# Newton steps of all inverse square roots moved from VectorE to GpSimd in a two-layer decoder

## The chip, the core and the metric

The kernel runs on one core of one Trainium2 chip. The metric is the device time of one execution in microseconds. A core has five engines that run their own instruction streams side by side and wait for one another by semaphores: TensorE (PE in the profile, with PEld for its weight loads), VectorE (DVE), ScalarE (ACT), GpSimd (POOL) and SyncE (SP), which here issues the DMAs.

## The reference, cut to what matters

The model has two pre-norm layers on 256 tokens of width 2048, with 16 heads of 128. Layer A is latent attention: a projection gives query and key/value latents and a gate, the latents are normalised and projected up per head, and queries and keys are normalised again before the scores. Layer B is plain attention here (one block of 256 keys) with a linear position bias, and with normalised queries and keys. All of these norms are

```python
def rms_norm(x, g):
    xf = x.astype(jnp.float32)
    y = xf * lax.rsqrt(jnp.mean(xf * xf, axis=-1, keepdims=True) + EPS)
    return (y * g.astype(jnp.float32)).astype(x.dtype)
```

The kernel has one inverse square root per token and norm to compute, a few numbers on each of the 128 partitions: 2, 6, 8 or 12 columns.

## The kernel before, in words

Every product is made of three passes (high times high, and two mixed ones) over parts of the operands. A weight block `wr` comes in by DMA; ScalarE rounds it to its high part `wh` (line 146) and VectorE subtracts that to get the low part `wl` (line 150, 128 x 1024 numbers in most cases). There are three buffers for `wl`, four for `wh`. TensorE's order is written out: a planner (`ordered`) merges a main list of projections with a side list of attention steps, and `chain` ties each matmul to the one ahead of it. So TensorE takes its work in one fixed order and, when an operand is late, waits. The order on the other engines is set by the compiler's scheduler, which estimates what is ready; each engine takes its own instructions strictly in the order that it was given.

The inverse square root is the function `rsqrt`. Two integer instructions make a first guess from the bits of the number (lines 303 and 304, here called the seed), then three Newton steps of three instructions follow (lines 306 to 308), each depending on the one before. It is called 19 times:

- `token_scale`, once for each layer (2 columns): the factor per token, copied to `r_a` or `r_b`, from which `diag` and the matmul `ps_r` make the factors by row.
- `lat_norm` (6 columns), once: the norms of the latents. After it VectorE scales `sf` (line 552), and TensorE transposes that (`ps_lt`).
- `kv_done` in `group_a` (12 columns), once for each of the 8 groups of two heads of layer A. After it VectorE makes `rp`, `tok`, `ra` and `rb` out of the projections in PSUM (lines 636 to 515), which TensorE transposes (`ps_ta`).
- `n_done` in `group_b` (8 columns), twice for each of the 4 groups of four heads of layer B. After it VectorE makes `tok` (line 786), which is transposed by DMA and split.

In layer A the projections follow each other as: query block (two `wl` of 768), key/value block (one `wl` of 1024), the rest of one gate (three `wl` of 1024) and the start of the next gate (one `wl` of 1024). The first is announced by the transposes `ps_ta`. The softmax of two heads of the group before (`sm`, `mn`, `ri`, `pz`) lies on VectorE and ScalarE in between.

Of the kernel before, what the change touches and what calls it, by code (L numbers as in the profile page):

```python
# [26 lines left out]
ALU = mybir.AluOpType  # L27
# [65 lines left out]
def trunk(ctx: ExitStack, tc, xT, gains, cst, w_in_a, w_q_up, w_kv_up, w_out_a, w_in_b, w_out_b, outT):  # L93
    nc = tc.nc
# [204 lines left out]
    def rsqrt(v, n, tag):  # L299

        y = wk.tile([P, n], F32, tag=tag + "y", name="rs_y")
        t = wk.tile([P, n], F32, tag=tag + "t", name="rs_t")
        nc.vector.tensor_scalar(y.bitcast(I32), v.bitcast(I32), 1, None, op0=ALU.logical_shift_right)
        nc.vector.tensor_scalar(y.bitcast(I32), y.bitcast(I32), -1.0, float(0x5F3759DF), op0=ALU.mult, op1=ALU.add)
        for _ in range(3):
            nc.vector.tensor_tensor(t, v, y, op=ALU.mult)
            nc.vector.scalar_tensor_tensor(t, t, -0.5, y, op0=ALU.mult, op1=ALU.mult)
            nc.vector.scalar_tensor_tensor(y, t, 1.5, y, op0=ALU.add, op1=ALU.mult)
        return y

    def split_x(c, gcol):
# [21 lines left out]
    def token_scale(ssq, lay, out, needs, more):  # L333


        def f():
            ps = work("ps_st")
            for t in range(2):
                matmul(ps[:, t * P:(t + 1) * P], ssq[:, t * P:(t + 1) * P], ones, start=True, stop=True)
            v = one.tile([P, 2], F32, name="rv_" + lay)  # L340
            nc.vector.tensor_scalar(v, ps[:, :2 * P:P], 1.0 / DM, EPS, op0=ALU.mult, op1=ALU.add)
            r = out["r"] = one.tile([P, 2], F32, name="r_" + lay)
            nc.vector.tensor_copy(r, rsqrt(v, 2, "x"))
            more()

        def g():
            pr = work("ps_r")
            d = wk.tile([P, S], F32, tag="og", name="diag")
            for t in range(2):
                nc.vector.tensor_scalar(d[:, t * P:(t + 1) * P], ident, out["r"][:, t:t + 1], None, op0=ALU.mult)  # L350
            matmul(pr[:, :S], ones, paired(d), start=True, stop=True)
            rows = out["rows"] = one.tile([P, S], F32, tag="rr", name="rr_" + lay)
            nc.vector.tensor_copy(rows, pr[:, :S])

        a = Step(f, 436, 5500, needs, bank=True)
        return a, Step(g, 436, 1500, [a], bank=True)
# [178 lines left out]
    def lat_norm():  # L535
        st = one.tile([P, 2, 3], F32, name="lat_st")
        v = one.tile([P, 2, 3], F32, name="lat_v")
        parts = ((0, QR), (QR, KVR), (QR + KVR, ROPE))
        for t in range(2):
            for i, (o, n) in enumerate(parts):  # L540
                sq = wk.tile([P, 512], F32, tag="gx", name="sq")
                nc.scalar.activation(sq[:, :n], lat[t][:, o:o + n], AF.Square,  # L542
                                     accum_out=st[:, t, i:i + 1])
        for i, (o, n) in enumerate(parts):
            nc.vector.tensor_scalar(v[:, :, i], st[:, :, i], 1.0 / n, EPS, op0=ALU.mult, op1=ALU.add)
        r = rsqrt(v.rearrange("p a b -> p (a b)"), 6, "l")
        krz = wk.tile([P, 384], F32, tag="sm", name="krz", bufs=3).rearrange("p (t a d) -> p t a d", t=2, a=3)
        nc.vector.memset(krz, 0.0)
        rp = wk.tile([P, 2, 1, ROPE], F32, tag="rp", name="rp", bufs=1)
        for t in range(2):  # L550
            for i, (o, n) in enumerate(parts[:2]):
                nc.vector.tensor_scalar(lat[t][:, o:o + n], lat[t][:, o:o + n], r[:, 3 * t + i:3 * t + i + 1], None,
                                        op0=ALU.mult)
            o = parts[2][0]
            nc.scalar.activation(rp[:, t, 0], lat[t][:, o:o + ROPE], AF.Copy, scale=r[:, 3 * t + 2:3 * t + 3])
        rope_of(rp, 2, 1, krz[:, :, 1:2])
        lat_st["krz"] = krz
# [42 lines left out]
    def group_a(g):  # L600
# [13 lines left out]
        def kv_done(a):  # L614
            st = z["st"]
            z["v"] = vh, vl, v1 = v_tiles()
            for t in range(2):
                v = a[t].rearrange("p (h d) -> p h d", h=2)
                for h in range(2):
                    sq = wk.tile([P, P], F32, tag="sqa", name="sqa", bufs=1)  # L620
                    nc.scalar.activation(sq, v[:, h, :P], AF.Square, accum_out=st[:, 1, t, h:h + 1])
                if t == 0:
                    split_v(vh[:, :2], vl[:, :2], v[:, :, P:], None)
                else:
                    nc.scalar.copy(v1[:, :2], v[:, :, P:])
            sf = st.rearrange("p a b c -> p (a b c)")
            var = wk.tile([P, 12], F32, tag="ga_v", name="ga_v")
            nc.vector.tensor_scalar(var[:, :8], sf[:, :8], 1.0 / P, EPS, op0=ALU.mult, op1=ALU.add)
            nc.vector.tensor_scalar(var[:, 8:], sf[:, 8:], 1.0 / ROPE, EPS, op0=ALU.mult, op1=ALU.add)
            f = rsqrt(var, 12, "ga").rearrange("p (a b c) -> p a b c", a=3, b=2)  # L630
            rp = wk.tile([P, 2, 2, ROPE], F32, tag="rp", name="rp", bufs=1)
            for t in range(2):
                tk = z["tok", t] = wk.tile([P, 512], F32, tag="tok", name="tok", bufs=4)
                q = z["q"][t].rearrange("p (h d) -> p h d", h=2)
                k = a[t].rearrange("p (h d) -> p h d", h=2)
                nc.vector.tensor_tensor(rp[:, t], q[:, :, P:], f[:, 2, t].unsqueeze(2).to_broadcast([P, 2, ROPE]),
                                        op=ALU.mult)
                for i, src in ((0, q), (1, k)):
                    nc.vector.tensor_tensor(tk[:, 256 * i:256 * (i + 1)].rearrange("p (h d) -> p h d", h=2), src[:, :, :P],
                                            f[:, i, t].unsqueeze(2).to_broadcast([P, 2, P]), op=ALU.mult)  # L640
            z["rope"] = rope_of(rp, 0, 2)
# [300 lines left out]
```

## Time and profile before

| | us |
|---|---|
| median of 3 runs | 756.62 |
| lowest and highest | 755.7, 757.58 |
| the profiled execution | 756.45 |
| its span, first to last instruction | 754.7 |
| outside the span | 1.75 |
| TensorE busy in the span | 745.3 (99%) |
| VectorE busy | 576.7 (76%) |
| ScalarE busy | 488.7 (65%) |
| GpSimd busy | 0.2 |

The share of busy time says which engine has work at all; whether a millisecond or a nanosecond on another engine reaches the end is told by TensorE's own waits, which the rows below list.

### The profile page before, as it was taken

To read this page: it belongs to the slowest core of one execution; us is meant where nothing else is said; L and a number is where in the kernel's file an instruction comes from. 1 tells how busy PE (TensorE), PEld (TensorE's weight loads), DVE (VectorE), ACT (ScalarE), POOL (GpSimd) and SP (SyncE) were. 2 spreads that over 40 slices of the span, in tenths; PEclk is the share of its full clock that TensorE was granted. 3 is DMA by queue.
4 is the path that set the end of the run, shared out by engine and by line. 5 is a ranking of instruction groups with operands and counts; after the bars stand their busy time and mean duration, and the time that the engine had idled before them with its cause. 6 is when DMAs were issued, how large, how long until landed. Compare 5 with 4: busy or idle time off the path is not lost.

```text
span 754.7 us, 14125 instructions
## 1 busy us (share of the span) xinstructions
PE 745.3 (99%) x5246; PEld 707.1 (94%) x5246; DVE 576.7 (76%) x1207; ACT 488.7 (65%) x1025; POOL 0.2 (0%) x4
## 2 busy tenths in 40 slices
PE   8999999999999999999999999999999999999997
PEld 7999999999999999998889988998889988899997
DVE  6888899999998596765787767886788857887552
ACT  7767888888877575445666556675567666674331
POOL 0000000000000000000000000000000000000000
PEclk9999999999999999999999999999999999999999
DMA  9866666666657966666877768876787677877761
GB/s 296 263 182 182 169 184 161 184 170 158 182 178 192 280 209 211 195 181 211 227 224 187 194 216 228 246 187 195 203 237 219 190 215 214 235 197 219 232 223 43
DMA packets 137973, 153.19 MB, mean 203 GB/s; under 512 B 47280, under 2 KB 94768, under 8 KB 137904
## 3 DMA queue, kind: packets, MB, share of 16 engines
q1 hardware_dynamic: 137760, 152.27, 70.4%
q8 instruction: 41, 0.67, 0.4%
q14 instruction: 28, 0.23, 0.1%
q10 hardware_dynamic: 144, 0.02, 0.0%
HBM read 139.68 MB, written 2.10 MB: 188 GB/s over the span
## 4 chain that ended last, share of the span: by engine, by line
PE 91%; DVE 4%; DMA 2%; ACT 1%; issue 1%; SPq 0%; DVEq 0%; ACTq 0%
PE acc L198 84%; PE ps_s L198 4%; DVE wl L150 2%; PE ps_o L198 2%; PE ps_ta L201 1%; DMA c_sb<-cst 1%; DMA wr<-w_in_a 1%; ACT wh L146 1%; DMA sm<-pz 0%; ACT sq L542 0%; DVE xt L724 0%; SPq L132 0%; PE ps_lt L201 0%; DVE xt L865 0%; DVE xl L314 0%
## 5 line engine op out<-in xcount | busy, mean ns | idle before, releaser
L146 ACT ACTIVATE wh<-wr 128x1024 fp32r<-128x1024 f32 (+3 forms) x265 | 287.9, 1091 | 161.8 <-PE acc L198 134.9
L150 DVE TENSOR_TENSOR wl<-wr,wh 128x1024 fp32r<-128x1024 f32 (+3 forms) x265 | 314.3, 1189 | 90.3 <-PE acc L198 58.1
L198 PE MATMUL acc<-wh,xh 128*128 128x512 f32 (+1 forms) x448 | 169.0, 377 | 1.2 <-ACT wh L146 1.2
L198 PE MATMUL acc<-wl,xh 128*128 128x512 f32 (+1 forms) x448 | 167.7, 374 | 0.8 <-DVE wl L150 0.8
L198 PE MATMUL acc<-wh,xl 128*128 128x512 f32 (+1 forms) x448 | 167.4, 374 | 0.0
L198 PE MATMUL acc<-xh,wh 128*128 128x256 f32 x512 | 142.3, 278 | 0.0
L198 PE MATMUL acc<-ogh,wh 128*128 128x256 f32 x512 | 142.0, 277 | 0.0
L198 PE MATMUL acc<-ogh,wl 128*128 128x256 f32 x512 | 141.0, 275 | 0.3 <-DVE wl L150 0.2
L198 PE MATMUL acc<-xh,wl 128*128 128x256 f32 x512 | 140.8, 275 | 0.0
L198 PE MATMUL acc<-ogl,wh 128*128 128x256 f32 x512 | 140.8, 275 | 0.0
L198 PE MATMUL acc<-xl,wh 128*128 128x256 f32 x512 | 140.8, 275 | 0.0
L198 PEld LDWEIGHTS acc<-ogh,wl 128*128 128x128 f32 x512 | 98.3, 192 | 0.7 <-DVE wl L150 0.7
L198 PEld LDWEIGHTS acc<-xl,wh 128*128 128x128 f32 x512 | 98.2, 192 | 0.3
L198 PEld LDWEIGHTS acc<-xh,wh 128*128 128x128 f32 x512 | 98.2, 192 | 0.3
L198 PEld LDWEIGHTS acc<-xh,wl 128*128 128x128 f32 x512 | 98.3, 192 | 0.0
L198 PEld LDWEIGHTS acc<-ogl,wh 128*128 128x128 f32 x512 | 98.3, 192 | 0.0
L198 PEld LDWEIGHTS acc<-ogh,wh 128*128 128x128 f32 x512 | 98.3, 192 | 0.0
L198 PEld LDWEIGHTS acc<-wh,xh 128*128 128x128 f32 x448 | 85.0, 190 | 11.9 <-ACT wh L146 1.9
L198 PEld LDWEIGHTS acc<-wl,xh 128*128 128x128 f32 x448 | 84.9, 190 | 11.4 <-DVE wl L150 1.3
L198 PEld LDWEIGHTS acc<-wh,xl 128*128 128x128 f32 x448 | 84.8, 189 | 10.3
L198 PE MATMUL acc<-wh,xt 128*128 128x384 f32 (+1 forms) x192 | 57.5, 357 | 0.0
L426 ACT ACTIVATE sm<-sm,mn 128x128 f32<-128x128 f32 x64 | 29.0, 455 | 11.3 <-DVE mn L424 11.3
(154 smaller groups left out, 833.5 us busy)
## 6 DMA issues: line engine op xcount, KB each, us to landing
wr<-w_in_b SPq DMA_DIRECT2D x128, 512.0 KB, 4.3
wr<-w_in_a SPq DMA_DIRECT2D x32, 512.0 KB, 4.1
wr<-w_out_a SPq DMA_DIRECT2D x32, 512.0 KB, 4.5
wr<-w_out_b SPq DMA_DIRECT2D x32, 512.0 KB, 4.6
wr<-w_in_a SPq DMA_DIRECT2D x15, 416.0 KB, 5.2
wr<-w_q_up SPq DMA_DIRECT2D x16, 384.0 KB, 3.8
wr<-w_kv_up SPq DMA_DIRECT2D x8, 512.0 KB, 3.8
xt<-xT SPq DMA_DIRECT2D x4, 512.0 KB, 5.5
```

The costliest lines, as they stand in the source:

```text
L146: nc.scalar.activation(self.ordering(self.h)[1], self.ordering(self.raw)[0], AF.Copy)
L150: nc.vector.tensor_tensor(self.ordering(self.l)[1], self.ordering(self.raw)[0], self.ordering(self.h.bitcast(F32))[1], op=ALU.subtract)
L198: chain(nc.tensor.matmul(*args, skip_group_check=True, **kw))
L201: chain(nc.tensor.transpose(*args))
L426: nc.scalar.activation(sm[:, sl], sm[:, sl], AF.Exp, bias=mn[:, t:t + 1], scale=-1.0, accum_out=rs[:, t:t + 1])
```

## The change

The three Newton steps go to GpSimd, where each has four instructions instead of three, since the fused form of lines 307 and 308 is written out. The seed stays on VectorE. The result `rs_y` is read by VectorE and ScalarE as before.

```diff
         for _ in range(3):
-            nc.vector.tensor_tensor(t, v, y, op=ALU.mult)
-            nc.vector.scalar_tensor_tensor(t, t, -0.5, y, op0=ALU.mult, op1=ALU.mult)
-            nc.vector.scalar_tensor_tensor(y, t, 1.5, y, op0=ALU.add, op1=ALU.mult)
+            nc.gpsimd.tensor_tensor(t, v, y, op=ALU.mult)
+            nc.gpsimd.tensor_tensor(t, t, y, op=ALU.mult)
+            nc.gpsimd.tensor_scalar(t, t, -0.5, 1.5, op0=ALU.mult, op1=ALU.add)
+            nc.gpsimd.tensor_tensor(y, y, t, op=ALU.mult)
         return y
```

The file has one line more behind line 308, so that what was line 552 is now 553. TensorE's order is the same instruction by instruction. On VectorE the order changes around each call. The call of `lat_norm` on VectorE before (`lat_v` are the variances, `sf_124` and `sf_125` the latents of the two token halves):

```order
L303 TENSOR_SCALAR rs_y<-lat_v 128x6
L304 TENSOR_SCALAR rs_y<-rs_y 128x6
L150 TENSOR_TENSOR wl<-wr,wh 128x1024
L306 TENSOR_TENSOR rs_t<-lat_v,rs_y 128x6
L307 SCALAR_TENSOR_TENSOR rs_t<-rs_t,rs_y 128x6
L308 SCALAR_TENSOR_TENSOR rs_y<-rs_t,rs_y 128x6
...
L552 TENSOR_SCALAR sf_124<-sf_124,rs_y 128x512
```

The same place on VectorE after the change:

```order
L303 TENSOR_SCALAR rs_y<-lat_v 128x6
L304 TENSOR_SCALAR rs_y<-rs_y 128x6
L150 TENSOR_TENSOR wl<-wr,wh 128x1024
L553 TENSOR_SCALAR sf_124<-sf_124,rs_y 128x512
L553 TENSOR_SCALAR sf_124<-sf_124,rs_y 128x256
```

One `wl` stands between the seed and the first reader of the result; the nine Newton instructions are gone from here. What stands for them on GpSimd, the first of three steps (the first row waits for VectorE, each later one for the row above it):

```order
L306 TENSOR_TENSOR rs_t<-lat_v,rs_y 128x6
L307 TENSOR_TENSOR rs_t<-rs_t,rs_y 128x6
L308 TENSOR_SCALAR rs_t<-rs_t 128x6
L309 TENSOR_TENSOR rs_y<-rs_y,rs_t 128x6
L306 TENSOR_TENSOR rs_t<-lat_v,rs_y 128x6
```

A call in a group of layer A (`kv_done`), on VectorE before, from the third group to the sixth word for word and in the seventh with a narrower `wl`:

```order
L304 TENSOR_SCALAR rs_y<-rs_y 128x12
L431 TENSOR_SCALAR sm<-sm,ri 128x256
L306 TENSOR_TENSOR rs_t<-ga_v,rs_y 128x12
L424 ISA sm,mn<-ps_s,c_sb 128x256
...
L429 RECIPROCAL ri<-rs 128x2
L307 SCALAR_TENSOR_TENSOR rs_t<-rs_t,rs_y 128x12
L150 TENSOR_TENSOR wl<-wr,wh 128x1024
L308 SCALAR_TENSOR_TENSOR rs_y<-rs_t,rs_y 128x12
L431 TENSOR_SCALAR sm<-sm,ri 128x128
L636 TENSOR_TENSOR rp<-acc,rs_y 128x128
```

The same place after:

```order
L304 TENSOR_SCALAR rs_y<-rs_y 128x12
L432 TENSOR_SCALAR sm<-sm,ri 128x256
L425 ISA sm,mn<-ps_s,c_sb 128x256
L425 ISA mn 128x1
L637 TENSOR_TENSOR rp<-acc,rs_y 128x128
...
L514 TENSOR_TENSOR rb<-rp,rope_t 128x4x32
L430 RECIPROCAL ri<-rs 128x2
L150 TENSOR_TENSOR wl<-wr,wh 128x1024
L516 TENSOR_TENSOR ra<-ra,rb 128x256
L432 TENSOR_SCALAR sm<-sm,ri 128x128
L432 TENSOR_SCALAR sm<-sm,ri 128x256
```

The reciprocal, the `wl` and the scaling of `sm`, which stood ahead of the first reader `rp`, now stand behind the last of the block that it opens (`rp`, `tok`, `rp`, `tok`, `ra`, `rb`, `rb`).

## Rows read from the trace of the kernel before

**Rows 1.** The page's first part: busy time, share of the span, instructions.
```profile
PE 745.3 (99%) x5246; PEld 707.1 (94%) x5246; DVE 576.7 (76%) x1207; ACT 488.7 (65%) x1025; POOL 0.2 (0%) x4
```

**Rows 2.** Waits of TensorE from 20 to 755 us: total, times, longest.
```profile
PE acc L198 <- DVE wl L150: 1.3, 6, 0.3
PE ps_lt L201 <- DVE sf L552: 0.3, 1, 0.3
PE ps_s L198 <- DVE sr L392: 0.3, 1, 0.3
```

**Rows 3.** Instructions on the tile rs_y: ns minimum, median, maximum; starts; forms.
```profile
L307 DVE SCALAR_TENSOR_TENSOR rs_t<-rs_t,rs_y x57: 154/167/174, 40.4 to 646.1; 128x12 f32<-128x12 f32 x24, 128x8 f32<-128x8 f32 x24, 128x2 f32<-128x2 f32 x6, 128x6 f32<-128x6 f32 x3
...
L304 DVE TENSOR_SCALAR rs_y<-rs_y x19: 152/171/174, 40.0 to 643.4; 128x12 int32<-128x12 int32 x8, 128x8 int32<-128x8 int32 x8, 128x2 int32<-128x2 int32 x2, 128x6 int32<-128x6 int32 x1
```

**Rows 4.** Timeline, first call: start us, length us, instruction, idle before it.
```profile
39.96 0.17 DVE L304 TENSOR_SCALAR rs_y<-rs_y 128x2 int32<-128x2 int32 x1
...
42.98 0.17 DVE L343 COPY r_a<-rs_y 128x2 f32<-128x2 f32 x1
...
43.18 0.61 ACT L528 ACTIVATE sf<-acc,r_a 128x416 f32<-128x416 f32 x1 [1.12 <-DVE r_a L343]
```

**Rows 5.** Timeline, the call of lat_norm and TensorE behind it.
```profile
50.10 0.17 DVE L304 TENSOR_SCALAR rs_y<-rs_y 128x6 int32<-128x6 int32 x1
...
53.12 0.59 ACT L555 ACTIVATE rp<-sf,rs_y 128x64 f32<-128x64 f32 x2 [2.63 <-DVE rs_y L308]
...
54.33 0.44 PE L201 MATMUL ps_lt<-c_sb,sf 128*128 128x128 f32 x2 [0.31 <-DVE sf L552]
```

**Rows 6.** Timeline of VectorE, the call of the third group of layer A.
```profile
110.89 0.17 DVE L304 TENSOR_SCALAR rs_y<-rs_y 128x12 int32<-128x12 int32 x1
...
112.96 1.22 DVE L150 TENSOR_TENSOR wl<-wr,wh 128x1024 fp32r<-128x1024 f32 x1
...
114.37 0.28 DVE L636 TENSOR_TENSOR rp<-acc,rs_y 128x128 f32<-128x128 f32 x1
...
116.63 0.29 DVE L513 TENSOR_TENSOR rb<-rp,rope_t 128x128 f32<-128x128 f32 x1
...
120.83 0.61 DVE L409 COPY pz<-sm 128x768 uint16<-128x768 uint16 x1 [0.16 <-DMA sm<-pz]
...
123.12 0.75 DVE L392 SCALAR_TENSOR_TENSOR sr<-ps_ta,g_sb,sr 128x512 fp32r<-128x512 f32 x1 [0.33 <-ACT sr L391]
...
123.99 2.35 DVE L150 TENSOR_TENSOR wl<-wr,wh 128x1024 fp32r<-128x1024 f32 x2
```

**Rows 7.** Timeline of TensorE in the same stretch.
```profile
117.31 0.28 PE L198 MATMUL acc<-xh,wl 128*128 128x256 f32 x1
...
125.26 0.48 PE L198 MATMUL acc<-wl,xt 128*128 128x512 f32 x1 [0.18 <-DVE wl L150]
```

**Rows 8.** Timeline, layer B: the end of the first key block's work, and its reader.
```profile
391.99 1.42 DVE L811 SCALAR_TENSOR_TENSOR sr<-flip,g_sb,sr 128x512 fp32r<-128x512 f32 x2
...
397.63 0.39 PE L198 MATMUL ps_s<-sf,sf 128*128 128x128 f32 x2
```

**Rows 9.** Timeline, the call of token_scale for layer B.
```profile
317.52 0.17 DVE L304 TENSOR_SCALAR rs_y<-rs_y 128x2 int32<-128x2 int32 x1
...
321.01 0.48 DVE L350 TENSOR_SCALAR diag<-c_sb,r_b 128x128 f32<-128x128 f32 x2
...
324.21 0.43 PE L198 MATMUL ps_r<-diag,ones 128*128 128x256 f32 x1
```

**Rows 10.** Groups by line and shape: busy us, mean ns, idle before.
```profile
L426 ACT ACTIVATE sm<-sm,mn 128x256 f32<-128x256 f32 x32 | 16.3, 508 | 2.5 <-DVE mn L424 2.5
...
L426 ACT ACTIVATE sm<-sm,mn 128x128 f32<-128x128 f32 x32 | 12.9, 403 | 8.7 <-DVE mn L424 8.7
...
L935 POOL MEMSET const-float32-0.0<- 128x1 f32 x1 | 0.1, 98 | 0.2 <-issue 0.2
```

## The prediction

> **What bounds the kernel now.** I read the page's busy shares first: TensorE 99%, VectorE 76%, ScalarE 65%, GpSimd nothing [rows 1]. The reader is to see that there is next to nothing to win. TensorE's order is fixed, and in its list of waits the whole stretch after 20 us holds 1.3 + 0.3 + 0.3 = 1.9 us [rows 2]. A lighter VectorE can give back these 1.9 us at most. So the question is only what the change makes late. I then went to the places where VectorE is already just in time for TensorE. There are two kinds. In the prologue TensorE stands 0.31 us for the scaled latents `sf`, which come straight out of the call of `lat_norm` [rows 5]. In each middle group of layer A it stands some 0.2 us for the `wl` of the key/value block [rows 7], which VectorE writes at the end of a run of work from 110.89 to 123.99 that has only 0.16 + 0.33 us of idle time in it [rows 6]. In layer B VectorE is ahead.
>
> **What goes and what comes.** Gone from VectorE: 19 calls of nine instructions, 171 in all, of about 0.167 us [rows 3], which follow each other at about 0.2 us, 1.8 us for a call without other work. New on GpSimd: 19 x 12 = 228 instructions, each waiting for the one before. Let T be the time from the end of the seed to the result, as its readers see it. Before, from the seed's end (39.96 + 0.17) to the reader `r_a` at 42.98, it is 2.85 us with one `wl` inside [rows 4], the same 2.85 from 50.10 + 0.17 to 53.12 [rows 5], and from 111.06 to `rp` at 114.37 it is 3.31 us with more inside [rows 6].
>
> **The price of a GpSimd step.** The trace has no GpSimd arithmetic. From below: a memset of one column took 98 ns [rows 10]; with some 0.03 us between it is 0.13 us, T = 12 x 0.13 + 0.1 for the two hand-offs = 1.7 us. Then the sequence on VectorE's 0.20 us: T = 2.5. From above: a slow short instruction is ScalarE's exponential, 508 ns on 256 columns [rows 10], with 0.03 us between 0.54: T = 6.6. Between these I take 0.40, the same exponential on 128 columns (403 ns, [rows 10]), as nearest: it also runs through a result that has to be written before the next may start, on an engine with a longer step than VectorE's. So **T = 12 x 0.40 + 0.1 = 4.9 us**. The Trainium skill's GPSIMD Engine Reference (section 3, Performance versus the Vector engine) calls GpSimd the wrong place for ordinary elementwise work and gives it 1.96 times VectorE's time at 2048 columns; no run here shows it. As an estimate from that page, 1.96 x 0.20 = 0.39 us, and the sum would be nearly the one below.
>
> **The prologue, two calls in a row.** `r_a` is what ScalarE waits for (1.12 us idle ahead of `sf`, [rows 4]), its `sf` feeds the squares, these the call of `lat_norm`, this `sf` again and `ps_lt`, for which TensorE already stands [rows 5]. No slack lies in between, so both delays add: 2 x (4.9 - 2.85) = **4.1 us**. The `wl` after the seed fills VectorE's time while it waits, but what is queued behind the reader (`diag`, two further `wl`) is late with it; that makes TensorE stand a little earlier, inside the same 4.1 us.
>
> **Layer A, five groups of one pattern.** The order on VectorE decides. After the seed stand only `sm` and one pass of the softmax, some 0.7 us, then `rp`, which waits for GpSimd; all behind it waits too. Behind it now stand its block up to `rb` (114.37 to about 116.83, 2.46 us), the reciprocal (0.15) and the `wl` that used to be written at 112.96, ahead of it [rows 6]. That `wl` is the one for the next gate: TensorE reads it first at 117.31 [rows 7], 13 steps after the key/value block. It would end at 111.06 + T + 2.46 + 0.15 + 1.22 = 114.9 + T, so TensorE stands T - 2.4 = 2.5 us. The same counted at the `wl` of 123.99: the reader comes T - 3.31 later, 1.5 us of work has moved behind it, and 0.5 us of idle time takes up part: T - 2.3, the same delay seen again, not a second one. Once TensorE has stood, VectorE is in step with it again, so the delay comes once in each group: 5 x 2.5 = **12.5 us**. The removed Newton work is in this already.
>
> **The other three calls of layer A.** The first group has idle time behind it, the second and the last have the `wl` ahead of the reader still. From 0 to 2.5 us each; I take 1, so **3 us**.
>
> **Layer B.** The call of `token_scale`: the second `diag`, which ended at 321.49, now comes after T, some 1.0 us of small instructions and a `wl`, at 317.69 + T + 2.2; `ps_r` wants it at 324.21 [rows 9]. It stands T - 4.3 = **0.6 us**. The eight calls of `n_done` have one `wl` ahead of the reader, as in the prologue, and shift by 2.05 us; the key block's last part is ready at 393.41 and read at 397.63 [rows 8]. These 4.2 us, and the `wl` buffers written ahead, hide it: **0**, until T passes 2.85 + 4.2 = 7.1. That a weight load now stands between the two transposing DMAs of a block on SP's queue is inside the same slack.
>
> **Sum.** 4.1 + 12.5 + 3 + 0.6 = 20.2 us on the profiled execution's 756.45 (span 754.7 and 1.75 outside; its median of three is 756.62): **777 us**.
>
> **Rivals.**
> - *GpSimd is as quick as VectorE (not slower).* The place is the step: at 0.20 us T is 2.5, the prologue gives back its 0.31, the five groups cost 0.1 each, and the time is 756.6. The memset row speaks for it, but it reads nothing and is not chained. It decides from a step of 0.23 us down (T = 2.9: 0.1 + 2.5, at the edge of what can be told). A gain beyond that edge can't be: only 1.9 us of waiting are there, 754.5.
> - *GpSimd is locked out by VectorE.* If GpSimd can't read while VectorE runs an instruction with two inputs from SBUF, the first Newton instruction waits for the `wl` behind the seed, 1.14 us. That costs 2.3 us in the prologue and up to 3.4 in the three other calls of layer A; the five groups have no such instruction there, layer B hides it. I take 4: 781 us. Afterwards VectorE stands still itself, so it can't lock out more. Nothing in the profile speaks for or against it, as GpSimd never ran beside VectorE. The Trainium skill's page SBUF — State Buffer (section Who interferes with whom) states it as a rule: the later of the two is blocked in full; no run here shows it yet.
> - *The step is longer than 0.52.* Each 0.1 us more is 1.2 us of T, and some 12 us of time. At 0.54 (T = 6.6): 7.5 + 5 x 4.2 + 6 + 2.3 = 37, 793 us. Beyond T = 7.1 layer B joins with eight calls: at 7.7 it is about 808.
>
> **How the numbers follow.** Under 0.3% (2.3 us) a measurement can't tell this kernel from no change. The likeliest case is a step from 0.30 to 0.52 without the lock: 0.45, time 766 to 791. With the lock 0.17, 770 to 795. A step of 0.23 to 0.30: 0.07, 759 to 766. As quick as VectorE: 0.14, 755 to 759, the same. Longer than 0.52: 0.15, 791 and up. Faster by over 0.3%: 0.02, which leaves something for an order that works out better than I see. So slower 0.84, same 0.14, faster 0.02. The range 757 to 806 leaves out some 0.09 at either end.
>
> **What would show it.** Right: GpSimd starts of one call some 0.4 us apart; VectorE idle ahead of `rp`, `r_a` and the scaling of `sf`, released by GpSimd; TensorE's waits grown to some 20 us, two thirds of them for `wl` in layer A, 2 to 3 us once per group, and 4 us at `ps_lt` or at a `wl` shortly before; layer B without waits. Wrong: a step near 0.2 us, where all of it vanishes; the first instruction of each call stretched until a `wl` ends, which is the lock; waits of TensorE for `sr` or `ps_s` in layer B, where my slack would be wrong; or waits in layer A that add up from both `wl` places instead of being one.

## The result, and the profile after

The changed kernel takes 788.24 us (median of six, 785.34 to 790.15) against 756.16 for the kernel before (six, 755.52 to 757.58): a ratio of 1.041, interval 1.039 to 1.043. It is slower, as forecast, by 32 us where the sum said 20. The execution profiled after took 789.15 us, with a span of 787.4. The page's first part answers to [rows 1]:

```profile
PE 755.7 (96%) x5246; PEld 713.4 (91%) x5246; DVE 552.9 (70%) x1036; ACT 485.5 (62%) x1025; POOL 59.3 (8%) x232
```

VectorE lost 23.8 us of work, GpSimd took 59. TensorE's waits from 20 to 785 us (total, times, longest), for [rows 2]:

```profile
PE acc L198 <- DVE wl L150: 14.6, 15, 2.3
PE ps_lt L201 <- issue: 3.0, 1, 3.0
PE ps_s L198 <- DVE sr L393: 2.8, 2, 2.3
PE ps_o L198 <- DVE sr L393: 1.7, 2, 1.1
PE acc L198 <- DVE tok L640: 0.8, 1, 0.8
PE ps_lt L201 <- DVE sf L553: 0.3, 1, 0.3
```

That is 23.2 us where it was 1.9. The first call, to be held against [rows 4] (timeline: start, length, instruction, idle time before it; GpSimd, then VectorE):

```profile
41.87 0.19 POOL L306 TENSOR_TENSOR rs_t<-rv_a,rs_y 128x2 f32<-128x2 f32 x1 [41.42 <-DVE rs_y L304]
...
42.42 0.19 POOL L308 TENSOR_SCALAR rs_t<-rs_t 128x2 f32<-128x2 f32 x1
42.69 1.22 POOL L309 TENSOR_TENSOR rs_y<-rs_y,rs_t 128x2 f32<-128x2 f32 x1
44.00 0.19 POOL L306 TENSOR_TENSOR rs_t<-rv_a,rs_y 128x2 f32<-128x2 f32 x1
...
42.64 1.23 DVE L150 TENSOR_TENSOR wl<-wr,wh 128x1024 fp32r<-128x1024 f32 x1 [0.85 <-PE acc L198]
46.16 0.17 DVE L344 COPY r_a<-rs_y 128x2 f32<-128x2 f32 x1 [2.29 <-POOL rs_y L309]
```

Two things stand here. A GpSimd step takes 0.27 to 0.28 us from start to start (0.28 to 0.30 with 12 columns), not 0.40. And one instruction, the one that started 0.05 us after the `wl`, took 1.22 us and ended with it. So T (from the end of the seed to the reader) is 4.37 us here. In all 13 calls with a `wl` beside the chain exactly one instruction is stretched in this way, and T is 4.27 to 4.65; in the six calls without one none is, and T is 3.54 (five groups of layer A) and 3.34 (two columns).

The call of the third group, for [rows 6, 7] (GpSimd's first and last instruction, then VectorE, ScalarE and TensorE):

```profile
119.81 0.24 POOL L306 TENSOR_TENSOR rs_t<-ga_v,rs_y 128x12 f32<-128x12 f32 x1 [18.32 <-DVE rs_y L304]
...
123.03 0.21 POOL L309 TENSOR_TENSOR rs_y<-rs_y,rs_t 128x12 f32<-128x12 f32 x1
...
123.27 0.29 DVE L637 TENSOR_TENSOR rp<-acc,rs_y 128x128 f32<-128x128 f32 x1 [2.94 <-POOL rs_y L309]
...
125.81 1.21 DVE L150 TENSOR_TENSOR wl<-wr,wh 128x1024 fp32r<-128x1024 f32 x1
...
127.26 0.55 DVE L432 TENSOR_SCALAR sm<-sm,ri 128x128 f32<-128x128 f32 x2
...
132.08 0.61 DVE L410 COPY pz<-sm 128x768 uint16<-128x768 uint16 x1 [0.51 <-DMA sm<-pz]
...
134.37 0.75 DVE L393 SCALAR_TENSOR_TENSOR sr<-ps_ta,g_sb,sr 128x512 fp32r<-128x512 f32 x1 [0.73 <-ACT sr L392]
...
135.23 2.35 DVE L150 TENSOR_TENSOR wl<-wr,wh 128x1024 fp32r<-128x1024 f32 x2
...
132.78 0.40 ACT L440 CAST ph<-pz 128x256 fp32r<-128x256 f32 x1 [1.26 <-DVE pz L410]
...
133.66 0.68 ACT L392 ACTIVATE sr<-ps_ta,g_sb 128x512 fp32r<-128x512 f32 x1
...
127.07 0.38 PE L198 MATMUL acc<-xh,wl 128*128 128x256 f32 x1 [0.92 <-DVE wl L150]
136.50 0.48 PE L198 MATMUL acc<-wl,xt 128*128 128x512 f32 x1 [1.56 <-DVE wl L150]
```

VectorE stands 2.94 us for GpSimd. The gate's `wl` (125.81) is late, and TensorE stands 0.92 us for it. But 9 us later it stands again, 1.56 us, for the key/value `wl`. The prediction had taken these two for one delay. From seed to seed the third, fourth and fifth group now take 24.8 to 25.0 us instead of 22.3, and the sixth, with a lower clock of TensorE in it (below), 27.1.

TensorE's clock, which the prediction left out, shows in windows of the same trace (start and end, length, busy time of PE, PEld, DVE, ACT, POOL with counts, granted clock, DMA share, GB/s):

```profile
52.00:58.40 6.40, 3.43 (x32) 3.27 (x30) 2.59 (x8) 2.27 (x10) 3.32 (x12) 1.00 0.45 145
58.40:62.20 3.80, 3.49 (x17) 3.30 (x18) 3.72 (x11) 2.46 (x4) 0.00 (x0) 0.55 0.17 16
...
212.20:215.80 3.60, 3.03 (x10) 2.58 (x11) 2.41 (x4) 3.29 (x15) 0.00 (x0) 0.53 0.45 125
...
260.00:266.90 6.90, 5.90 (x27) 5.79 (x28) 5.17 (x16) 4.21 (x10) 0.00 (x0) 0.51 0.55 165
```

Late in a wait or just behind it (that of 2.97 us at `ps_lt`, one of 2.31 us for a `wl`, one of 2.33 us for `sr`) the granted clock goes to the lower level (1.2 GHz), and stays there for 3.4, 3.4 and 6.8 us. Half of that, 6.8 us together, is the most that it can have cost, since TensorE still waited in part of these stretches. Counted by how far the matmuls behind the three waits fall back against the kernel before, it is 1.4 + 1.4 + 2.8 = 5.6 us. The kernel before had no such stretch between 20 and 750 us.

Where the time went, from the starts of the seeds in both traces, the lower clock taken out as half of its stretches:

| stretch | on record | measured | clock besides |
|---|---|---|---|
| up to the first seed | 0 | 1.65 | |
| prologue, two calls | 4.1 | 2.7 | 1.7 |
| five groups of layer A | 12.5 | 13.5 | 1.7 |
| the other three calls of layer A | 3 | 4.3 | 3.4 |
| layer B | 0.6 | 3.7 | |
| sum | 20.2 | 25.9 | 6.8 |

The first line is a lower clock at start-up, ahead of the first Newton instruction on GpSimd. The executions of the kernel before that ran beside the experiments differ in the same way (757.3 to 762.0 us at a mean granted clock of 0.995 to 0.998, 755.6 to 757.3 at 0.999 or 1.000), so I count it to the spread. Two runs below that leave GpSimd idle, the four-instruction form and the order alone, begin with the same stretch of 3.4 us. The stretches lose more than the waits listed in them: across a listed wait of 0.92 us the matmuls fall 1.09 us further behind those of the kernel before. If the clock is taken as 5.6 us, the other 1.2 us of its column belong to the waits.

### The profile page after: what moved, and what is told of

It reads as the page before. It is cut to its first block, busy times and chain, and to the rows that moved or that the text cites. A ratio compares the mean times of both kernels' runs of the same rounds, so it can differ in the third digit from the quotient of the medians.

```text
span 787.4 us, 14183 instructions
## 1 busy us (share of the span) xinstructions
PE 755.7 (96%) x5246; PEld 713.4 (91%) x5246; DVE 552.9 (70%) x1036; ACT 485.5 (62%) x1025; POOL 59.3 (8%) x232
## 4 chain that ended last, share of the span: by engine, by line
PE 67%; DVE 11%; ACT 6%; DMA 5%; POOL 5%; issue 4%; SPq 0%; DVEq 0%; ACTq 0%
PE acc L198 63%; DVE wl L150 4%; DMA sm<-pz 3%; PE ps_o L198 2%; DMA tok<-flip 2%; PE ps_s L198 2%; ACT wh L146 2%; POOL rs_y L309 2%; POOL rs_t L306 1%; POOL rs_t L307 1%; DVE tok L640 1%; POOL rs_t L308 1%; DMA wr<-w_in_a 1%; ACT sqa L622 1%; DVE sm L432 0%
## 5 line engine op out<-in xcount | busy, mean ns | idle before, releaser
L150 DVE TENSOR_TENSOR wl<-wr,wh 128x1024 fp32r<-128x1024 f32 (+3 forms) x265 | 313.4, 1188 | 86.1 <-PE acc L198 63.1
L198 PE MATMUL acc<-wl,xt 128*128 128x384 f32 (+1 forms) x96 | 34.5, 360 | 8.3 <-DVE wl L150 8.2
```

Source lines behind the costliest of these rows:

```text
L150: nc.vector.tensor_tensor(self.ordering(self.l)[1], self.ordering(self.raw)[0], self.ordering(self.h.bitcast(F32))[1], op=ALU.subtract)
L198: chain(nc.tensor.matmul(*args, skip_group_check=True, **kw))
```

## The experiments

The theory: VectorE takes its instructions in order, so that all behind the first reader of `rs_y` waits for GpSimd's chain, TensorE waits in turn, and its clock falls behind some of these waits. The rivals: the fourth instruction of a step is what costs; GpSimd's traffic slows the others wherever it runs; the clock falls for reasons of its own.

### The four-instruction form on VectorE

```diff
-            nc.gpsimd.tensor_tensor(t, v, y, op=ALU.mult)
+            nc.vector.tensor_tensor(t, v, y, op=ALU.mult)
             ...
```

> All 228 Newton instructions in the four-instruction form, but on VectorE. Theory of the queue (VectorE is held behind the reader of rs_y for as long as GpSimd's chain of 12 takes, 3.4 us, or 4.3 to 4.6 with a wl beside it, and all that stands behind the reader is late): no engine is handed to, other work fits between the steps, so nearly nothing: 756 to 759 us, TensorE's waits after 20 us under 5 us. Rival of the form (the fourth instruction is what costs): 57 more instructions of 0.167 us are 9.5 us of VectorE, 766 us if all of it reached the end.

765.43 us, ratio 1.010 (1.009 to 1.012). My theory missed, and the rival of the form came close: 57 instructions more cost 7.8 to 8.9 us with GpSimd idle (by the profiled execution without a lower clock at start-up, and by the medians). TensorE stood 1.9 + 0.4 us at `ps_lt`, and the middle groups grew by 0.2 to 0.6 us, where a call has three instructions of 0.2 more. But the run does not separate these instructions from the order, which changed with them: in the prologue a `wl` now stands ahead of the seed of `lat_norm`, and in the third group the reader `rp` comes 4.93 us behind the seed where it came 3.32, with more of the softmax ahead of it. What it shows is that VectorE's run of work in the prologue and in layer A has little slack beside the 0.16 + 0.33 us of idle time in [rows 6]. In the changed kernel the fourth instruction costs VectorE nothing; on GpSimd it makes three of the twelve steps of T.

### One part of the calls at a time

```diff
+            if tag in ("x", "l"):      # then ("ga",), then ("gb",)
                 nc.gpsimd...
+            else:
+                nc.vector...           # three instructions, as before
```

> GpSimd only for the calls of token_scale (two) and lat_norm; the other 16 as before. Theory of the queue: the two prologue calls have a wl beside them, T is 4.4, so 2 x (4.4 - 2.85) = 3.1 us of waiting at ps_lt, nothing at the third call; behind that wait some 3.4 us at the lower clock, 1.7 us more: 756.2 + 4.8 = 761 us. By the sum on record 756.2 + 4.1 + 0.6 = 760.9 without any change of the clock. Rival of the traffic (GpSimd's accesses slow the other engines wherever it runs, in proportion to the calls): 3 of 19 x 32 = 5 us, but spread over the stretches and with longer VectorE instructions, not as one wait. Rival of a clock of its own (the granted clock falls for another reason than TensorE's wait): no lower clock behind ps_lt, 759.3.

> GpSimd only for the eight calls of kv_done. Theory of the queue: the waits that the changed kernel has from 80 to 262 us come back, some 17 us of them, and with them the lower clock behind the longest of them (two or three stretches of 3.4 us, 3 to 5 us of time): 756.2 + 17 + 4 = 777, 773 to 780. By the sum on record 12.5 + 3 = 15.5, 771.7. Rival of the traffic: 8 of 19 x 32 = 13.5, 769.7. Rival of a clock of its own: 773 without a stretch at the lower clock.

> GpSimd only for the eight calls of n_done. Theory of the queue, with the order on SP as second part (a weight load stands between the two transposing DMAs of a block and holds the second): the three waits of layer B come back, 0.2 + 1.4 + 1.0 = 2.6 us, 758.8; they are for a wl that VectorE writes behind its wait for the second transposing DMA. By the sum on record 0: 756.2. Rival of the traffic: 8 of 19 x 32 = 13.5, 769.7.

The calls of `token_scale` and `lat_norm`: 762.07 us, ratio 1.006 (1.004 to 1.008). `ps_lt` waits 2.94 us with the lower clock for 3.4 us behind it, as in the changed kernel; the call for layer B costs nothing, where the sum had 0.6. Another wait, of 1.26 us for a `wl` at 199 us, stands in the sixth group of layer A, whose Newton steps are on VectorE here; what makes it is not shown.

Layer A: 778.15 us, ratio 1.027 (1.026 to 1.029). All its waits are back (0.91 for the gate's `wl`, 1.4 to 2.3 for the next one). But the clock did not follow. The window behind its wait of 2.31 us:

```profile
206.00:208.20 2.20, 0.00 (x0) 0.00 (x1) 2.13 (x4) 2.17 (x9) 0.00 (x0) 1.00 0.03 7
208.20:211.60 3.40, 3.40 (x19) 3.11 (x20) 2.31 (x5) 3.09 (x15) 0.00 (x0) 1.00 0.59 174
```

So the length of one wait does not decide whether the clock falls, and layer A costs some 19 us by its waits alone (so far do the matmuls fall back in it).

Layer B: 759.24 us, ratio 1.003 (1.002 to 1.005), some 2.6 us as expected and not 0, though the profiled execution shows only 0.6 us of listed waits there, where I had expected 2.6 (its matmuls fall 2.1 us back). A share by the number of calls (13.5 us for eight) is excluded here, and with it the rival of the traffic; in the changed kernel, too, the mean `wl` takes VectorE 1188 ns, before it was 1189. The three parts make 3.6% together, the whole 4.1%.

### Two Newton steps instead of three

```diff
-        for _ in range(3):
+        for _ in range(2):
```

> All calls on GpSimd, but with two Newton steps instead of three; the third step of every inverse square root is left out, so eight instructions in a chain instead of twelve. Theory of the queue: T is 8 x 0.28 + 0.1 = 2.4 us, 3.4 with a wl beside it. Prologue 2 x (3.4 - 2.85) = 1.1, no wait left for the gate's wl in the middle groups (T - 2.4 = 0), some 0.5 us in each of four groups for the key/value wl, 1 us in the others, nothing in layer B: 756.2 + 4 = 760, and no lower clock, since no wait comes near 2 us. Rival of the traffic (GpSimd's accesses as such cost, in proportion to their number): two thirds of 32 us stay, 777.

772.46 us, ratio 1.019 (1.016 to 1.022): neither 760 nor 777. T is 2.38 us in the middle groups, less than the 3.31 of the kernel before, and still the third and fifth group take 24.0 us instead of 22.3, and the fourth, with the lower clock in it, 24.8. Their gate waits are gone, as T - 2.4 = 0 said. What stayed is the second wait:

```profile
PE acc L198 <- DVE wl L150: 7.1, 7, 1.5
PE ps_o L198 <- DVE sr L393: 2.6, 2, 1.6
```

So the second wait is not the stand of VectorE at `rp` passed on. It needed another cause. The clock missed my expectation as well: it went to the lower level twice for 3.4 us, once behind a wait of 1.45 us in the fourth group, while a wait of 1.45 us in the third had none behind it.

### The readers later

```diff
+    def held(ins):
+        for prior in ("sm", "wl"):
+            if prior in res:
+                after(ins, res[prior])
...
-                nc.vector.tensor_tensor(rp[:, t], q[:, :, P:], ...)
+                held(nc.vector.tensor_tensor(rp[:, t], q[:, :, P:], ...))
```

with the block from `rp` to `rb` written out a little later, so that reciprocal, `wl` and both scalings of `sm` stand ahead of it, as before the change.

> All calls on GpSimd as in the changed kernel; only VectorE's order changes in the middle groups: reciprocal, gate wl and the scaling of sm stand ahead of rp and tok again. TensorE's order is the same. Theory of the queue: the four waits for the gate's wl (0.9 each, 3.7 us) go, and the key/value waits (1.6 to 2.3 us) get shorter by the work that now lies inside VectorE's wait, 1.22 + 0.15 + 0.5 us, less the 1.0 us by which this wl locks GpSimd out: some 0.9 each. 788.2 - 3.7 - 3.6 = 781, and 1.7 to 3.4 us less where the lower clock goes with them: 777 to 782. Rival of the traffic: as many GpSimd instructions beside as much work, 788.

775.33 us, ratio 1.024 (1.021 to 1.026), 13 us less than the changed kernel and more than expected; up to 3.4 of them are the clock, which has two stretches of 3.4 us at the lower level left. The gate waits are gone, and those for the key/value `wl` are down to 0.3 us. VectorE in the third group:

```profile
120.15 1.22 DVE L150 TENSOR_TENSOR wl<-wr,wh 128x1024 fp32r<-128x1024 f32 x1
...
123.09 0.29 DVE L646 TENSOR_TENSOR rp<-acc,rs_y 128x128 f32<-128x128 f32 x1 [1.26 <-POOL rs_y L309]
```

T is longer here, 4.68 us, since the `wl` now runs beside the chain (one GpSimd instruction takes 1.16 us) and the scaling of `sm` too (the next takes 0.38), and the groups take 22.9 to 23.2 us all the same. Of the kernels with all calls on GpSimd the one with the longer T has the shorter groups: what stands behind the reader costs more than the wait itself.

### The order alone, without GpSimd

The kernel before, with its reciprocal of the second head and that `wl` tied behind `rb`:

```diff
-            nc.vector.reciprocal(ri, rs)
+            inv = nc.vector.reciprocal(ri, rs)
+            if "rb" in res and h % 2 and cost > 600:
+                after(inv, res["rb"])
```

> The kernel before, Newton steps of three instructions on VectorE, GpSimd idle; only VectorE's order in the middle groups is that of the changed kernel: the reciprocal, the gate wl and the scaling of the second head's sm stand behind rp, tok, ra and rb. Theory of the order (the second wait of a group, for the key/value wl, comes from the second head's softmax, which is started later, and not from the length of GpSimd's chain): the reader comes some 2.4 us behind the seed, no wait for the gate's wl, but one of about 1.4 us for the key/value wl in each of four or five groups, as in the run with two Newton steps: 756.5 + 6 to 8 = 763 to 765 us. Rival of the length (only the time that VectorE stands for GpSimd counts): nothing stands here, 756 to 758.

763.93 us, ratio 1.008 (1.005 to 1.011). The time is as expected, its place is not: the second to the fifth group lost less than 0.4 us each, the first and the last three 1.0 to 1.7 each. So the order on VectorE alone does not make the second wait of the middle groups, which is 0.2 to 0.5 us here. With nearly the same order on VectorE and nearly the same T as the run with two steps (2.23 and 2.38 us), the third and fifth group are 1.7 us shorter. The two traces differ in ScalarE's order: here both `sr` stand ahead of the second head's `ph`, there `ph` stands ahead of both and ScalarE stands 1.5 to 1.6 us at it for `pz`; in the changed kernel `ph` stands between them. That suggested the next run.

### ScalarE's order

The changed kernel; the second head's `ph` and `p1` behind the key block's `sr`:

```diff
-            nc.scalar.copy(ph, pz[:, :S])
+            c = nc.scalar.copy(ph, pz[:, :S])
+            if "rest" in st and "part" in res:
+                behind(c, res["part"])         # part: the sr of the key block
```

> The changed kernel, all calls on GpSimd, with ScalarE's order turned in the middle groups: the second head's ph and p1, which wait for the transposed pz, stand behind the two sr of queries and keys instead of between them; VectorE's pl moves one place with them. If the second wait of a group comes from ScalarE standing for the late pz with sr queued behind it: VectorE's 0.7 us of idle time ahead of the key block's sr goes, the key/value wl is written some 0.9 us earlier, and its waits in four groups shrink from 1.6 to 2.3 us to 0.7 to 1.4: 788.2 - 4 = 784, and 1.7 to 3.4 us less if a stretch at the lower clock goes too: 780 to 784. If the second wait is only the stand of VectorE at rp passed on: it stays, 788.

779.35 us, ratio 1.030 (1.029 to 1.032), 9 us less than the changed kernel, up to 3.4 of them through the clock, which has 6.8 us less at the lower level. The rows that answer to those of the changed kernel at 132.08 to 135.23:

```profile
130.05 0.61 DVE L412 COPY pz<-sm 128x768 uint16<-128x768 uint16 x1 [0.46 <-DMA sm<-pz]
...
130.93 0.75 DVE L394 SCALAR_TENSOR_TENSOR sr<-ps_ta,g_sb,sr 128x512 fp32r<-128x512 f32 x1
...
132.12 2.36 DVE L150 TENSOR_TENSOR wl<-wr,wh 128x1024 fp32r<-128x1024 f32 x2
...
129.79 0.69 ACT L393 ACTIVATE sr<-ps_ta,g_sb 128x512 fp32r<-128x512 f32 x1
130.76 0.41 ACT L455 CAST ph<-pz 128x256 fp32r<-128x256 f32 x1 [0.28 <-DVE pz L412]
```

The `sr` is written before ScalarE comes to `ph`, VectorE does not stand for it, and from `pz` to the key/value `wl` it takes 2.07 us instead of 3.15. TensorE's waits there fell from 1.6 to 0.4 to 0.6 in three groups and from 2.3 to 1.2 in the fourth; the gate waits (0.91) stayed. The third to the fifth group take 23.7 to 23.8 us instead of 24.8 to 25.0. This settles most of the second wait: `sm` is scaled late (127.26), its transpose is back late (132.08), ScalarE stands 1.26 us for it at `ph`, and the `sr` queued behind `ph` holds VectorE ahead of the `wl`.

### Matmuls into the wait at `ps_lt`

```diff
+            if b == 0:
+                for _ in range(50):
+                    matmul(ps[:, :P], ones_b, ones_b, start=True, stop=True)
```

> The changed kernel, with 50 matmuls of 128 columns that compute nothing of use ahead of the first transposes ps_lt, where TensorE stands 3.0 us. At the higher clock they take about 3 us. Theory that the clock falls because TensorE stood: behind ps_lt the granted clock stays at 2.4 GHz, where it was 1.2 GHz for 3.4 us, and the time is 1.7 us shorter: 786.5 us (less certain in the time than in the trace, since the changed kernel's runs lie between 785.3 and 790.2); the other stretches at the lower clock stay. Rival of a clock of its own: the stretch at 1.2 GHz stays in the trace, 788.2 or a little more.

785.52 us, ratio 1.037 (1.035 to 1.040): the time does not separate it from the changed kernel (1.039 to 1.043). The trace does:

```profile
55.34 2.97 PE L198 MATMUL ps_lt<-ones_b 128*128 128x128 bf16 x50
...
58.40:62.20 3.80, 3.41 (x29) 3.22 (x30) 3.80 (x12) 3.25 (x6) 0.00 (x0) 1.00 0.09 11
```

The granted clock is 1.00 instead of 0.55 in the same window, and the matmuls behind `ps_lt` fall back by 0.05 us instead of 1.43. Each of the five kernels here that waits 2.94 to 2.97 us at this place has the lower clock behind it; the one that works through the wait has not. At this place TensorE's standing is the cause. The other stretches did not stay as I had expected: the one of 3.4 us at 212 us is gone, but one of 6.8 us begins at 186 us, in a wait of 2.31 us. So the whole execution holds as much of the lower clock as that of the changed kernel, and the time of the whole does not show the 1.4 us that were won at `ps_lt`.

### The weight load between the transposing DMAs

```diff
+            if "both" in res:
+                after(load, res["both"])       # the second transposing DMA of the block
```

> GpSimd only for the eight calls of n_done, as in the run of layer B alone, but every weight load that followed is held on SP's queue behind the two transposing DMAs of a block, which so stand together again as before the change. If the load between them makes layer B's waits: they go, 756.2 to 757. If it is the longer T itself: 2.6 us stay, 758.8.

786.09 us, ratio 1.038 (1.035 to 1.040), far off both expectations. The tie held two loads more than meant, and ScalarE then waited for weights (its waits from 360 to 400 us, TensorE's from 300 to 760):

```profile
ACT wh L149 <- DMA wr<-w_in_b: 3.1, 5, 1.3
PE acc L201 <- ACT wh L149: 12.1, 8, 2.1
```

It tells nothing on the question, so it was asked again, with two loads let through and with the order of the run with the readers later:

> All calls on GpSimd, with VectorE's order in the middle groups as in the run with the readers later, and on SP's queue the one weight load that stood between the two transposing DMAs of a block held behind them (the two loads ahead of it are left alone, unlike in the run that held all). If the load between them makes layer B's waits: those of 0.2, 1.6 and 0.6 us go and the time is 775.3 - 2.4 = 773 us. If it is the longer T of the calls: they stay, 775.

774.52 us, ratio 1.022 (1.019 to 1.024), 0.8 us less than the run with the readers later where 2.4 were expected, and too near to its 1.024 to tell apart by time. In the trace the waits for `wl` in layer B fell from 2.4 us to 0.2 (another, of 0.4 for `ogh`, came at 709 us):

```profile
PE acc L202 <- ACT ogh L465: 0.4, 1, 0.4
PE acc L202 <- DVE wl L154: 0.2, 1, 0.2
```

VectorE's stand in the changed kernel, and TensorE's behind it, where the load lay between:

```profile
490.23 0.75 DVE L410 COPY flip<-tok 128x1024 uint16<-128x1024 uint16 x1 [3.11 <-DMA tok<-flip]
...
493.71 0.48 PE L198 MATMUL acc<-wl,xh 128*128 128x512 f32 x1 [1.42 <-DVE wl L150]
```

With the load behind both, the longest stand for such a transpose from 460 to 500 us is 1.02 us:

```profile
495.19 0.76 DVE L419 COPY flip<-tok 128x1024 uint16<-128x1024 uint16 x1 [1.02 <-DMA tok<-flip]
```

So the load makes these waits of layer B, at an unchanged T. It does not make most of the time lost there: the matmuls still fall 2.8 us back in layer B against the kernel before, where it was 3.4 with the load between. They lose it at other places, 0.9 us of it at `ogh`, and why is not shown.

### The price of a step by itself

The whole computation is left out; one chain of 12 instructions at a time, beside different work of VectorE.

> The whole computation is left out; the kernel only runs the chain of 12 GpSimd instructions, each time released by a VectorE instruction: alone with 2, 6, 8, 12, 64 and 256 columns, then with 12 columns beside VectorE instructions back to back: six wl (two inputs from SBUF, 128 x 1024), ten tensor_scalar and ten copies of 128 x 1024 (one input from SBUF), ten with one input from PSUM and one from SBUF, ten with PSUM alone; last beside six ScalarE activations. Theory: alone a step of 0.28 us from 2 to 12 columns, 3.4 us for the chain; beside the wl each starting instruction waits for the wl that runs, 1.0 to 1.2 us, so that the chain takes up to 3.4 + 6 x 1.1 = 10 us; beside PSUM inputs and ScalarE 3.4. For one input from SBUF the traces say little: 3.4 if only two-input instructions hold GpSimd up. The Trainium skill (SBUF — State Buffer, section Who interferes with whom) counts copy and tensor_scalar in their two-port modes among those that block: then 3.4 plus most of the ten instructions' time. Rival, that a chain is slow because of the hand-off between the engines and not because of the wl: 3.4 in every case.

There is one execution, with every case in it twice; the two agree within 0.02 us. First the chain beside six `wl`, of which VectorE's row is the fourth; then one row of the chain beside work with one input from PSUM:

```profile
35.12 1.12 POOL L149 TENSOR_TENSOR t_both<-v_both,y_both 128x12 f32<-128x12 f32 x1 [0.76 <-DVE y_both L145]
36.31 1.18 POOL L150 TENSOR_TENSOR t_both<-t_both,y_both 128x12 f32<-128x12 f32 x1
...
42.62 0.20 POOL L151 TENSOR_SCALAR t_both<-t_both 128x12 f32<-128x12 f32 x1
...
34.95 7.51 DVE L118 TENSOR_TENSOR wl<-wr,wh 128x1024 fp32r<-128x1024 f32 x6
...
61.98 0.21 POOL L149 TENSOR_TENSOR t_psum<-v_psum,y_psum 128x12 f32<-128x12 f32 x1 [0.76 <-DVE y_psum L145]
```

| chain of 12 | us |
|---|---|
| alone, 2 / 6 / 8 / 12 columns | 3.23 / 3.31 / 3.33 / 3.41 |
| alone, 64 / 256 columns | 4.50 / 8.61 |
| 12 columns, beside six `wl` | 9.15 |
| beside ten tensor_scalar, or ten copies, of 128 x 1024 from SBUF | 7.72 |
| beside ten instructions with one input, or the only one, from PSUM | 3.39 |

The activations ran beside the first chains of few columns instead, which took as long as later without them. Each `wl` lets one GpSimd instruction through when it ends. VectorE lost little: six `wl` took 7.51 us, 1.26 from start to start, where two in a row took 2.35 us in the changed kernel. The Trainium skill's page SBUF — State Buffer (section Who interferes with whom) has two inputs from SBUF lock GpSimd's reads out, and also copies and tensor_scalar in their two-port modes; the trace agrees, with 1.12 to 1.19 and 0.58 to 0.66 us for an instruction of 0.2 (no row names the mode that a copy ran in). The rival, the hand-off between the engines, falls with the 3.39 us beside work from PSUM, which has the same hand-off.

## Why the prediction was right, and where not

**The mechanism** was right: VectorE stands at the reader, in order, and TensorE stands for what is queued behind it. The way and the places (`ps_lt`, the gate's `wl` once per group, in four of the five groups) held. That the time lies in the stated range, 757 to 806, is in good part luck: with the measured T the prediction's own terms give 2 x (4.37 - 2.85) + 5 x (3.54 - 2.4) + 3 + 0 = 11.7 us, 768 us, and the step of 0.27 to 0.30 us that was measured had a chance of 0.07, at 759 to 766 (the lock had 0.17, but with the longer step). Most of the other 20 us are costs that it did not have: the second wait, the clock, layer B.

**T = 4.9 us** was too long. A step is 0.28 us, not 0.40; T is 3.34 to 3.54 without the lock and 4.27 to 4.65 with it. The exponential was the wrong neighbour; the memset's bound of 0.13 and VectorE's 0.20 lay on the other side.

**The lock**, a rival with 0.17, is there in all 13 calls that have a `wl` beside the chain. With T = 4.37 the prologue's formula gives 2 x (4.37 - 2.85) = 3.0 us; measured 2.7, and 2.94 at `ps_lt` with these calls alone. Its part in the prologue is about 2 us, 2 x (4.37 - 3.34), by the same formula; no run takes the lock away by itself.

**"The same delay seen again, not a second one"** is the step that failed in layer A. T - 2.4 gives 1.1 us a group for the gate's `wl`; 0.92 was listed and 1.09 lost. The second wait came on top, because the softmax of the second head had been moved behind the reader as well, and ScalarE and a DMA lie in its way: with the old order on VectorE it is 0.3 us, with ScalarE's order turned 0.4 to 0.6, where it was 1.6 to 1.7 in the same three groups. That the five groups came out near 12.5 is two errors that met: T too long by 1.4, and a wait missing by which 1.4 to 1.5 us are lost in a group.

**Layer B at 0** failed through the queue that the prediction named and waved through: the weight load between the transposing DMAs is not inside the slack. Removing it took the listed waits away at an unchanged T, but only 0.6 of the 3.4 us that were lost there; the rest of layer B's loss stays open. The 0.6 us of `token_scale` were not there, since T was 3.34 in that call and T - 4.3 is below zero.

**The clock** was in no term. It cost 5.6 to 6.8 us, more than any other line of the sum was off by.

**The floor** (nothing to win) held: no version here was as fast as the kernel before. The nearest, with the calls of layer B alone on GpSimd, took 759.24 us against 756.58.

Open: why waits of 2.3 us were followed by the lower clock in the changed kernel and not with layer A alone, and one of 1.45 us with two steps; why the last groups lose more than the middle ones; and where layer B loses its other 2.8 us.

## What to carry to other kernels

When a short chain is moved to another engine, price less the chain than what the scheduler puts behind its first reader: list the moved instructions on every engine and queue, and follow each to its own next reader, through ScalarE and the DMAs too. A long VectorE instruction with SBUF inputs beside a chain on GpSimd makes the chain longer by about its own time, but that can be worth it: the order with the `wl` beside the chain had the longer T and was 13 us faster than the one with the `wl` behind the reader. And where TensorE will stand for some microseconds, leave room in the sum for its clock.

## What was not expected of the hardware

- GpSimd's step hardly depends on the columns up to 12 (0.27 to 0.30 us from start to start), and a chain of 256 columns takes only 2.5 times as long (8.61 us).
- VectorE's copies and tensor_scalar of 0.69 us hold GpSimd up too, 0.58 to 0.66 us an instruction, while its work from PSUM, even with a second input from SBUF, costs GpSimd nothing.
- Behind a wait of 2.97 us TensorE ran 3.4 us at 1.2 GHz, and with matmuls of no use in that wait it did not. Behind a wait of 1.45 us the same happened once, and once it did not.
